# Zero rows of the decode tokens left out of DRAM and set on chip; z_b stored per block and channel in runs of 2 KB

## The chip, the cores and the metric

The kernel runs on one core of a Trainium2 chip. The metric is the device time of one execution in microseconds (us). Before the change it is 2897.08 us, the median of three runs (2893.88 to 2901.46).

## The reference, cut to what matters

One layer of a hybrid decoder, for 2048 prompt tokens and 8 decode tokens of one new position each, all in fp32. The layer projects the normalised input, mixes it in two branches, and projects back:

```
h    = rmsnorm(x, g_pre) * (1 + scale) + shift
u_a, v_a, z_a, x_b, z_b = split(h @ w_in)          # 5 x 1024 columns
y_a  = u_a * (tril(w_s) @ layernorm(v_a) + b_s) * silu(z_a)      # 8 heads, chunks of 128
h_t  = abar * h_(t-1) + bbar @ x_b[t]              # S5: 64 groups of 16 channels, 64 complex states each
g    = (Re(C h_t) + d * x_b[t]) @ w_glu + b_glu
y_b  = g[:16] * sigmoid(g[16:]) * silu(z_b)
out  = x + gate * rmsnorm(concat(y_a, y_b) @ w_out, g_post)
```

The prompt starts from a zero state. Each decode token starts from a given state and takes one step.

## The kernel before

**Blocks and column tiles.** The 2056 tokens stand on the free axis in four blocks (`blk`, `ranges`): 512 tokens in blocks 0 to 2, and 512 + 8 decode tokens in block 3, which is worked as 256 and 264 columns. TensorE multiplies in fp32r with both factors split in a high and a low part, so each product is three matmuls (`mm3`, L97 to L99). A column tile is 128 output channels of `h @ w_in`: 16 k-steps of three matmuls per range.

**Weights.** A half column tile of `w_in` (8 k-steps) comes in one 512 KB load into a raw tile `wraw` (L108; 3 buffers). ScalarE rounds it to `whi` (L90) and VectorE or GpSimd makes `wlo` (L85); there are 5 buffers (`NW`) of 4 k-steps each. A load waits for a free raw tile.

**Stages.** After the startup, the first stage makes x_b and z_b (8 column tiles of each, one per `e`), block by block from 0 to 3, up to about 870 us. `ev_xb` splits x_b in high and low parts and stores them to DRAM (`XB[e]`), ordered as channel, t, part, k, where a prompt token is 8k + t. `ev_zb` stores silu(z_b) (`ZB[e]`). Beside this stage `s5_mats` prepares the S5's matrices on GpSimd, ScalarE and VectorE in 16 rounds and stores them (PS, MQ, MT). The second stage makes v, z_a and u_a, block 3 first, then 0 to 2, up to about 2150 us, and the S5 runs inside it. The third stage is `@ w_out`.

**The S5.** Eight tokens (t) of 16 channels (c) are the 128 partitions of a tile, and k = 0 to 255 the columns; 8 further columns carry the decode tokens. `s5_u_mm` makes the state's inputs of a group from `xr` (128 x 2 x 272) and `pr`; `s5_scan` runs the recurrence over k on VectorE; `s5_y_load` loads, per group, `hr` (2 loads), `xr` again, `wr` (3 loads) and `zbl`; `s5_y_mm` does 12 matmuls, ScalarE, VectorE and GpSimd finish the tile `sg`, and it is stored to YB. In the S5's tiles a decode token is one column in which only one t is set: t = 7 where its inputs are made (columns 0 to 7 of the 272), t = 0 where its output is made (columns 264 to 271), and in `zbl` t = 0; the other seven rows are zero. The stores of block 3 (`dz`) write these columns to DRAM with their zeros, in runs of 8 numbers.

**What sets the order.** The code is emitted in program order by slots (`s5_steps`: 22 slots per `e`; in one half column tile of `phase1_rest` one slot is worked), and the tile framework then orders each engine's instructions by its own timeline model. Each engine runs its list in order; all DMAs are issued by SyncE (SP), in one list. There are eight DMA semaphores, used in turn, and a DMA waits until the one eight places before it has landed.

Of the kernel before, what the change touches and what calls it, by code (L numbers as in the profile page):

```python
# [28 lines left out]
GC = 16  # L29
P = 64  # L30
KT = D // 128
TC = 8
NK = L // TC
XW = NK + 2 * ND
HW = NK + ND
EPS = 1e-6
NE = 8
LEV = 5
MAGIC = 12582912.0
S5X, S5N = 4, 2  # L40
# [17 lines left out]
def ranges(b):  # L58

    return [(0, TB)] if b < NB - 1 else [(0, 256), (256, 264)]  # L60


class Builder:
# [330 lines left out]
    def ev_xb(self, b, e, acc):  # L394

        hi, lo = self.tile_(), self.tile_()
        hv, lv = (o[:, 0:TB].rearrange("p (t k) -> p t k", t=TC) for o in (hi, lo))
        for a, (r0, rn) in zip(acc, ranges(b)):
            m = min(rn, TB - r0)
            av = a[:, 0:m].rearrange("p (k t) -> p t k", t=TC)  # L400
            ks = slice(r0 // TC, (r0 + m) // TC)
            self.S.copy(hv[:, :, ks].bitcast(F32R), av)
            self.sub(self.V, lv[:, :, ks].bitcast(F32R), av, hv[:, :, ks])
        cols = slice(ND + b * 64, ND + b * 64 + 64)
        self.SP.dma_start(self.XB[e][:, :, 0, cols], hv)
        self.SP.dma_start(self.XB[e][:, :, 1, cols], lv)
        if b == NB - 1:
            dz = self.sp_.tile([128, 2, TC, 2, ND], F32, tag="dz", bufs=2, name=self.nm("dz"))
            self.G.memset(dz, 0.0)
            d = acc[1][:, 256:264]  # L410
            for i, t in ((0, TC - 1), (1, 0)):
                self.V.tensor_copy(dz[:, i, t, 0, :].bitcast(F32R), d)
                self.sub(self.V, dz[:, i, t, 1, :].bitcast(F32R), d, dz[:, i, t, 0, :])
            self.SP.dma_start(self.XB[e][:, :, :, 0:ND], dz[:, 0])
            self.SP.dma_start(self.XB[e][:, :, :, ND + NK : XW], dz[:, 1])

    def ev_zb(self, b, e, acc):
        o = self.tile_()
        ov = o[:, 0:TB].rearrange("p (t k) -> p t k", t=TC)
        for a, (r0, rn) in zip(acc, ranges(b)):  # L420
            m = min(rn, TB - r0)
            av = a[:, 0:m].rearrange("p (k t) -> p t k", t=TC)
            os_ = ov[:, :, r0 // TC : (r0 + m) // TC]
            self.S.activation(os_, av, AF.Sigmoid)
            self.V.tensor_mul(os_, os_, av)  # L425
        self.SP.dma_start(self.ZB[e].rearrange("t p k -> p t k")[:, :, b * 64 : b * 64 + 64], ov)
        if b == NB - 1:
            dz = self.sp_.tile([128, 2, TC, ND], F32, tag="dz", bufs=2, name=self.nm("dz"))
            self.G.memset(dz[:, 0], 0.0)
            self.S.activation(dz[:, 0, 0, :], acc[1][:, 256:264], AF.Sigmoid)  # L430
            self.V.tensor_mul(dz[:, 0, 0, :], dz[:, 0, 0, :], acc[1][:, 256:264])
            self.SP.dma_start(self.ZB[e].rearrange("t p k -> p t k")[:, :, NK:HW], dz[:, 0])

    def ev_v(self, b, j, acc):
        T, V, S = self.T, self.V, self.S
# [427 lines left out]
            SP.dma_start(mt[ti], kv[:, :, 32 * (TC - ti) : 32 * (TC - ti) + 256])  # L863


    def s5_x(self, e, gl):

        x = self.s5.tile([128, 2, XW], F32R, tag="s5x", bufs=S5X, name=self.nm("xr"))
        self.SP.dma_start(x.bitcast(F32), self.XB[e][gl * GC : gl * GC + GC].rearrange("c t h k -> (c t) h k"))
        return x  # L870

    def s5_u_load(self, e, gl):
        x = self.s5_x(e, gl)
        p = self.s5.tile([128, 2, 128], F32R, tag="s5p", bufs=S5N, name=self.nm("pr"))
# [75 lines left out]
    def s5_y_load(self, e, gl, r):  # L950
        SP, s5, nm = self.SP, self.s5, self.nm
        q, g2 = gl // 2, gl % 2
        h = s5.tile([128, 2, HW], F32R, tag="s5h", bufs=S5N, name=nm("hh"))
        self.split(r, h[:, 0], h[:, 1], self.V)
        x = self.s5_x(e, gl)
        w = s5.tile([128, 2, 2, 128, 2], F32R, tag="s5w", bufs=S5N, name=nm("wr"))
        mt = self.MT[e][gl // 4][q % 2].rearrange("t (h g c) n -> h g c t n", h=2, g=2)
        for hl in range(2):
            SP.dma_start(w[:, 0, hl].rearrange("p n e -> p (n e)").bitcast(F32), mt[hl, g2])
        SP.dma_start(w[:, 1].rearrange("p h n e -> p h (n e)").bitcast(F32), self.MQ[e][gl])  # L960
        zb = s5.tile([128, HW], F32, tag="s5z", bufs=S5N, name=nm("zbl"))
        SP.dma_start(zb, self.ZB[e][:, gl * GC : gl * GC + GC, :])
        return x, w, h, zb

    def s5_y_mm(self, e, gl, t):

        x, w, h, zb = t
        nm = self.nm
        g = e * 8 + gl
        mm = self.T.matmul  # L970
        xs = slice(ND, XW)
        po = []
        for hf in (1, 0):
            pg = self.ps.tile([128, 512], F32, tag="aux", bufs=4, name=nm("pg"))[:, 0:HW]
            po.append(pg)
            wm, wq = [w[:, 0, i, :, hf] for i in range(2)], [w[:, 1, i, :, hf] for i in range(2)]
            mm(pg, wm[0], x[:, 0, xs], start=True, stop=False)
            mm(pg, wm[0], x[:, 1, xs], start=False, stop=False)
            mm(pg, wm[1], x[:, 0, xs], start=False, stop=False)
            mm(pg, wq[0], h[:, 0, :], start=False, stop=False)  # L980
            mm(pg, wq[0], h[:, 1, :], start=False, stop=False)
            mm(pg, wq[1], h[:, 0, :], start=False, stop=True)
            if hf:
                yield
        sg = self.s5.tile([128, HW], F32, tag="sg", bufs=2, name=nm("sg"))
# [347 lines left out]
    def build(self):  # L1333
        nc, tc, I, V, G, SP = self.nc, self.tc, self.I, self.V, self.G, self.SP
# [29 lines left out]
        with tc.manual_schedule():  # L1364
            w, acc = self.startup(st, NG, nta)
# [186 lines left out]
```

## Time and profile before

| | |
|---|---|
| median of three runs | 2897.08 us |
| the profiled execution | 2893.71 us, span 2891.9 us, mean granted TensorE clock 0.995 |
| first stage (x_b, z_b) | to about 870 us |
| second stage (v, z_a, u_a and the S5) | about 870 to 2150 us |
| third stage (`@ w_out`) | about 2150 us to the end |
| DMA | 456704 packets, 581.22 MB |

The profile is of one execution. The engines are PE (TensorE's matmuls), PEld (its weight loads), DVE (VectorE), ACT (ScalarE), POOL (GpSimd) and SP (SyncE, which here only issues DMAs). The span runs from the first instruction to the last; some 2 us of the execution's time lie outside it. A busy PE is a PE with a matmul in flight; PEclk is the share of TensorE's full clock (2.4 GHz) that was granted.

### The profile page before, as it was taken

The numbers are of one execution on the slowest core, as the hardware profiler recorded it, in microseconds if no ns is written. First come the engines' busy times: TensorE is split into PE (matmuls) and PEld (weight loads), VectorE is DVE, ScalarE is ACT, GpSimd is POOL, SyncE is SP. The second block draws the span as 40 slices with busy tenths as digits, with TensorE's granted clock in tenths as the row PEclk, the third lists the DMA queues.
The fourth block names the chain that finished last, engine by engine and source line by source line (L and its number), as shares of the span: only waits on it lengthen the run. The fifth ranks groups of instructions, "written<-read, shape, count | busy, mean of one in ns | idle before, by whom it ended". The sixth has DMA issues, their size and how long they took to land.

```text
span 2891.9 us, 44349 instructions
## 1 busy us (share of the span) xinstructions
PE 2826.6 (98%) x15804; PEld 2375.1 (82%) x15804; DVE 1586.6 (55%) x2931; ACT 1065.5 (37%) x2008; POOL 1046.4 (36%) x973
## 2 busy tenths in 40 slices
PE   7999999999999999999999999999999999999998
PEld 4676777778899999988887888888888888888986
DVE  5467656465342837565546735482741174372866
ACT  3334444434233232433333332433243343434543
POOL 1128562662331232323232233223234345363443
PEclk9999999999999999999999999999999999999999
DMA  9898998987887373836476565637483365474676
GB/s 365 285 248 231 267 255 233 287 228 207 191 204 209 102 239 123 269 129 209 143 236 187 153 201 178 211 125 237 134 254 107 98 179 181 118 232 120 193 244 226
DMA packets 456704, 581.22 MB, mean 201 GB/s; under 512 B 216609, under 2 KB 303265, under 8 KB 456481
## 3 DMA queue, kind: packets, MB, share of 16 engines
q1 hardware_dynamic: 456482, 578.38, 66.9%
q8 instruction: 124, 2.03, 0.3%
q14 instruction: 98, 0.80, 0.1%
HBM read 466.94 MB, written 102.66 MB: 197 GB/s over the span
## 4 chain that ended last, share of the span: by engine, by line
PE 77%; DVE 10%; DMA 6%; issue 2%; SPq 2%; POOL 2%; ACT 1%; DVEq 0%; ACTq 0%; POOLq 0%
PE acc L97 23%; PE acc L99 23%; PE acc L98 22%; DVE Ub L899 2%; DVE wlo L85 2%; DMA wraw<-in_win 2%; PE ada L271 1%; DMA wraw<-in_woutr 1%; DVE sct L909 1%; DVE Ub L908 1%; DMA x<-in_xT 1%; DVE sct L907 1%; DVE Ub L910 1%; DMA wr<-MQ 1%; PE mix L531 1%
## 5 line engine op out<-in xcount | busy, mean ns | idle before, releaser
L97 PE MATMUL acc<-hi,whi 128*128 128x512 f32 (+2 forms) x3200 | 1132.6, 355 | 4.2 <-DVE t L425 2.6
L99 PE MATMUL acc<-hi,wlo 128*128 128x512 f32 (+2 forms) x3200 | 1121.2, 351 | 4.0 <-DVE wlo L85 3.7
L98 PE MATMUL acc<-lo,whi 128*128 128x512 f32 (+2 forms) x3200 | 1119.9, 350 | 3.8 <-DVE lo L375 3.5
L90 ACT CAST whi<-wraw 128x512 fp32r<-128x512 f32 x960 | 581.4, 620 | 1130.6 <-PE acc L98 796.4
L85 DVE TENSOR_TENSOR wlo<-wraw,whi 128x512 fp32r<-128x512 f32 x626 | 538.8, 867 | 826.0 <-ACT whi L90 794.8
L85 POOL TENSOR_TENSOR wlo<-wraw,whi 128x512 fp32r<-128x512 f32 x334 | 473.3, 1419 | 1054.7 <-ACT whi L90 960.6
L97 PEld LDWEIGHTS acc<-hi,whi 128*128 128x128 f32 x3200 | 604.1, 189 | 99.9 <-issue 19.4
L99 PEld LDWEIGHTS acc<-hi,wlo 128*128 128x128 f32 x3200 | 603.4, 189 | 91.2 <-DVE wlo L85 6.6
L98 PEld LDWEIGHTS acc<-lo,whi 128*128 128x128 f32 x3200 | 604.3, 189 | 80.2 <-DVE lo L375 6.7
L97 PE MATMUL acc<-yhi,whi 128*128 128x512 f32 (+1 forms) x1024 | 376.9, 369 | 2.8 <-DVE o L1074 2.8
L99 PE MATMUL acc<-yhi,wlo 128*128 128x512 f32 (+1 forms) x1024 | 375.0, 367 | 2.0 <-POOL wlo L85 2.0
L98 PE MATMUL acc<-ylo,whi 128*128 128x512 f32 (+1 forms) x1024 | 375.9, 367 | 0.0
L97 PEld LDWEIGHTS acc<-yhi,whi 128*128 128x128 f32 x1024 | 193.2, 189 | 38.4 <-DVE o L1074 3.6
L99 PEld LDWEIGHTS acc<-yhi,wlo 128*128 128x128 f32 x1024 | 192.8, 189 | 36.3 <-POOL wlo L85 2.4
L98 PEld LDWEIGHTS acc<-ylo,whi 128*128 128x128 f32 x1024 | 193.1, 189 | 34.5 <-issue 0.7
L899 DVE SCALAR_TENSOR_TENSOR Ub<-Ub,apow 128x128 f32<-128x128 f32 (+6 forms) x384 | 143.2, 438 | 2.5 <-ACT Ub L886 2.2
L988 POOL TENSOR_TENSOR sg<-sg,zbl 128x264 f32<-128x264 f32 x64 | 54.7, 854 | 192.3 <-DVE sg L987 124.6
L90 ACT CAST hh<-hr 128x264 fp32r<-128x264 f32 x64 | 26.3, 413 | 191.6 <-DMA hr<-Ub 97.5
L1077 POOL TENSOR_TENSOR ossq<-ossq,osq 128x512 f32<-128x512 f32 (+1 forms) x60 | 81.8, 1363 | 32.1 <-ACT osq L1070 31.9
L338 POOL TENSOR_TENSOR ssq<-ssq,t 128x512 f32<-128x512 f32 (+1 forms) x45 | 62.3, 1384 | 73.2 <-ACT t L337 72.5
L375 DVE SCALAR_TENSOR_TENSOR lo<-x,shiftT,hi 128x512 fp32r<-128x512 f32 x96 | 86.8, 921 | 0.7 <-ACT hi L374 0.5
L374 ACT ACTIVATE hi<-x,shiftT 128x512 fp32r<-128x512 f32 x96 | 67.3, 721 | 50.8 <-DVE x L373 42.9
(288 smaller groups left out, 2753.2 us busy)
## 6 DMA issues: line engine op xcount, KB each, us to landing
wraw<-in_win SPq DMA_DIRECT2D x320, 512.0 KB
wraw<-in_wout SPq DMA_DIRECT2D x128, 512.0 KB
xr<-XB SPq DMA_DIRECT2D x128, 272.0 KB
x<-in_xT SPq DMA_DIRECT2D x128, 256.0 KB
wraw<-in_wss SPq DMA_DIRECT2D x64, 512.0 KB
XB<-t SPq DMA_DIRECT2D x64, 256.0 KB
wraw<-in_wgt SPq DMA_DIRECT2D x32, 512.0 KB
MQ<-qh SPq DMA_DIRECT2D x128, 128.0 KB
```

Source lines behind the costliest of these rows:

```text
L85: eng.tensor_tensor(out, a, b, op=ALU.subtract)
L90: self.S.copy(hi, raw)
L97: mm(acc, whi, xhi, start=start, stop=False)
L98: mm(acc, whi, xlo, start=False, stop=False)
L99: mm(acc, wlo, xhi, start=False, stop=stop)
L271: self.T.matmul(ps[k * 32 : k * 32 + 32, 0:256], self.stat[:, q * 4 + k, :], raw[:, k * 256 : k * 256 + 256], start=q == 0, stop=q == 3)
L338: add_eng.tensor_tensor(ssq[:, 0:n], ssq[:, 0:n], sq[:, 0:n], op=ALU.add)
L374: S.activation(hi[:, 0:TB], xt, AF.Identity, bias=self.shiftT[:, k, 0:1])
L375: V.scalar_tensor_tensor(lo[:, 0:TB], xt, self.shiftT[:, k, 0:1], hi[:, 0:TB].bitcast(F32), op0=ALU.add, op1=ALU.subtract)
L899: V.scalar_tensor_tensor(o, i, f, o, op0=ALU.mult, op1=ALU.add)
L988: self.G.tensor_tensor(sg, sg, zb, op=ALU.mult)
L1077: eng.tensor_tensor(ssq[:, 0:nn], ssq[:, 0:nn], sq[:, 0:nn], op=ALU.add)
```

## The change

The decode columns of x_b and of silu(z_b) go to small DRAM tensors of their own, XD and ZD, without zeros. The S5's tiles have 264 columns where `xr` had 272: `s5_x` takes `tau` (7 for the input side, 0 for the output side), GpSimd sets the 8 decode columns of the tile to zero, one DMA loads the 256 prompt columns and another loads the 16 partitions of the decode columns that aren't zero. `ZB[e]` is now ordered as block, channel, t, k: a store writes 2 KB per channel, and a group's `zbl` is loaded in four DMAs of 32 KB, one per block, and one of ZD.

```diff
@@ ev_xb
-        cols = slice(ND + b * 64, ND + b * 64 + 64)
+        cols = slice(b * 64, b * 64 + 64)
...
-            dz = self.sp_.tile([128, 2, TC, 2, ND], F32, tag="dz", bufs=2, name=self.nm("dz"))
-            self.G.memset(dz, 0.0)
+            dz = self.sp_.tile([128, 2, ND], F32, tag="dz", bufs=2, name=self.nm("dz"))
             d = acc[1][:, 256:264]
-            for i, t in ((0, TC - 1), (1, 0)):
-                self.V.tensor_copy(dz[:, i, t, 0, :].bitcast(F32R), d)
-                self.sub(self.V, dz[:, i, t, 1, :].bitcast(F32R), d, dz[:, i, t, 0, :])
-            self.SP.dma_start(self.XB[e][:, :, :, 0:ND], dz[:, 0])
-            self.SP.dma_start(self.XB[e][:, :, :, ND + NK : XW], dz[:, 1])
+            self.V.tensor_copy(dz[:, 0, :].bitcast(F32R), d)
+            self.sub(self.V, dz[:, 1, :].bitcast(F32R), d, dz[:, 0, :])
+            self.SP.dma_start(self.XD[e], dz)
@@ ev_zb
-        self.SP.dma_start(self.ZB[e].rearrange("t p k -> p t k")[:, :, b * 64 : b * 64 + 64], ov)
+        self.SP.dma_start(self.ZB[e][b], ov)
...
-            dz = self.sp_.tile([128, 2, TC, ND], F32, tag="dz", bufs=2, name=self.nm("dz"))
-            self.G.memset(dz[:, 0], 0.0)
...
-            self.SP.dma_start(self.ZB[e].rearrange("t p k -> p t k")[:, :, NK:HW], dz[:, 0])
+            dz = self.sp_.tile([128, ND], F32, tag="dzz", bufs=2, name=self.nm("dz"))
...
+            self.SP.dma_start(self.ZD[e], dz)
@@ s5_x
-    def s5_x(self, e, gl):
-        x = self.s5.tile([128, 2, XW], F32R, tag="s5x", bufs=S5X, name=self.nm("xr"))
-        self.SP.dma_start(x.bitcast(F32), self.XB[e][gl * GC : gl * GC + GC].rearrange("c t h k -> (c t) h k"))
+    def s5_x(self, e, gl, tau):
+        x = self.s5.tile([128, 2, HW], F32R, tag="s5x", bufs=S5X, name=self.nm("xr"))
+        gs = slice(gl * GC, gl * GC + GC)
+        p0, d0 = (ND, 0) if tau else (0, NK)
+        xf = x.bitcast(F32)
+        self.G.memset(xf[:, :, d0 : d0 + ND], 0.0)
+        self.SP.dma_start(xf[:, :, p0 : p0 + NK], self.XB[e][gs].rearrange("c t h k -> (c t) h k"))
+        self.SP.dma_start(xf[tau::TC, :, d0 : d0 + ND], self.XD[e][gs])
@@ s5_y_load
-        SP.dma_start(zb, self.ZB[e][:, gl * GC : gl * GC + GC, :])
+        self.G.memset(zb[:, NK:HW], 0.0)
+        gs = slice(gl * GC, gl * GC + GC)
+        for b in range(NB):
+            SP.dma_start(zb[:, b * 64 : b * 64 + 64], self.ZB[e][b, gs].rearrange("c t k -> t c k"))
+        SP.dma_start(zb[0:GC, NK:HW], self.ZD[e][gs])
@@ build
+        self.XB = [dt_([128, TC, 2, NK], f"XB{e}") for e in range(NE)]
+        self.XD = [dt_([128, 2, ND], f"XD{e}") for e in range(NE)]
+        self.ZB = [dt_([NB, 128, TC, NK // NB], f"ZB{e}") for e in range(NE)]
+        self.ZD = [dt_([128, ND], f"ZD{e}") for e in range(NE)]
```

The order on GpSimd moves in block 3 of the first stage. Before, its list there holds the zeroing of `dz` (16 in all, L409 and L429) between the steps of `s5_mats` (F, mu, sc and ks are its tiles):

```order
L766 TENSOR_TENSOR dw_7216<-glw_7103,dd_7105 32x64
L409 MEMSET dz_7184 128x256
L766 TENSOR_TENSOR F_7375<-sc_7214,pw 128x576
L766 TENSOR_TENSOR mu_7195<-sc_7214,pw 128x576
L409 MEMSET dz_7354 128x256
L768 TENSOR_TENSOR F_7375<-F_7375,mu_7195 128x576
L824 TENSOR_SCALAR sc_7214<-sc_7214 128x128
L857 MEMSET ks_7556 64x2x256
```

After the change the same steps of the same round stand there alone:

```order
L761 TENSOR_TENSOR dw_7220<-glw_7111,dd_7113 32x64
L852 MEMSET ks_7552 64x2x256
L761 TENSOR_TENSOR F_7375<-sc_7218,pw 128x576
L761 TENSOR_TENSOR mu_7199<-sc_7218,pw 128x576
L763 TENSOR_TENSOR F_7375<-F_7375,mu_7199 128x576
L819 TENSOR_SCALAR sc_7218<-sc_7218 128x128
```

The 16 zeroings of `dz` are gone from GpSimd's list in the first stage; `ks` has moved ahead of the steps on F.

The order on SP moves where the S5's output groups are loaded. Before, between two loads of `wraw` in the S5 of `e` = 4, this is the beginning of the list (25 DMAs stand between the two loads):

```order
L108 DMA wraw_17613<-in_win 128x1024
L869 DMA xr_17602<-XB_61 128x544
L959 DMA wr_17467<-MT_0_137 128x1x256 x2
L960 DMA wr_17467<-MQ_125 128x512
L947 DMA hr_17543<-Ub 64x264
L989 DMA YB_77<-sg_17454 8x16x264
L962 DMA zbl_17471<-ZB_69 128x1x264
L959 DMA wr_17537<-MT_1_138 128x1x256 x2
L989 DMA YB_77<-sg_17521 8x16x264
```

After the change the same place reads as follows, and 49 DMAs stand between the two loads of `wraw`:

```order
L107 DMA wraw_17935<-in_win 128x1024
L869 DMA xr_17917<-XB_61 128x2x256
L960 DMA wr_17770<-MT_0_153 128x1x256 x2
L961 DMA wr_17770<-MQ_141 128x512
L948 DMA hr_17858<-Ub 64x264
L993 DMA YB_93<-sg_17755 8x16x264
L966 DMA zbl_17774<-ZB_77 128x1x64 x4
L967 DMA zbl_17774<-ZD_85 16x8
L993 DMA YB_93<-sg_17829 8x16x264
```

One load of `zbl` has become five, and each load of `xr` is followed, here or a few places on, by one of XD. SP's list has 2491 DMAs where it had 2115. In the S5 the longest stretch between two loads of `wraw` has 63 DMAs (it had 39; the first `e`), and in each of the seven other `e` there is one of 47 or 49 DMAs, where before three of them had one of 25 and none of the others had as many as 18.

On GpSimd's list in the second stage the zeroings of the decode columns (128 of `xr`, 64 of `zbl`) now stand between the products `sg` and the subtractions `wlo`:

```order
L992 TENSOR_TENSOR sg_11409<-sg_11409,zbl_11229 128x264
L963 MEMSET zbl_12562 128x8
L868 MEMSET xr_11532 128x2x8
L84 TENSOR_TENSOR wlo_11248<-wraw_11245,whi_11247 128x512
L868 MEMSET xr_11609 128x2x8
L992 TENSOR_TENSOR sg_11503<-sg_11503,zbl_11342 128x264
L84 TENSOR_TENSOR wlo_11358<-wraw_11355,whi_11357 128x512
```

Before, only the `sg`, the `wlo` and the products `t` of the gMLP stood there.

## Rows read from the trace of the kernel before

**Rows 1.** The page's first part: busy us, share of the span, instructions.
```profile
PE 2826.6 (98%) x15804; PEld 2375.1 (82%) x15804; DVE 1586.6 (55%) x2931; ACT 1065.5 (37%) x2008; POOL 1046.4 (36%) x973
```
**Rows 2.** Stretches of 50 us: busy us by engine, clock, DMA share, GB/s.
```profile
core 0: us, PE busy (x) PEld busy (x) DVE busy (x) ACT busy (x) POOL busy (x), PEclk, DMA share, GB/s
800.00:850.00 50.00, 46.21 (x368) 45.03 (x368) 22.94 (x37) 17.46 (x42) 26.53 (x34) 0.93 0.86 208
1000.00:1050.00 50.00, 49.71 (x413) 49.35 (x414) 25.71 (x63) 16.51 (x33) 16.72 (x15) 1.00 0.66 203
```
**Rows 3.** Stretches of 10 us within the first stage's end, same columns.
```profile
770.00:780.00 10.00, 5.67 (x47) 5.46 (x46) 4.77 (x6) 2.95 (x7) 7.32 (x7) 0.98 0.92 189
780.00:790.00 10.00, 8.72 (x70) 8.20 (x70) 3.70 (x12) 2.96 (x7) 5.23 (x11) 0.85 0.93 239
810.00:820.00 10.00, 6.21 (x42) 5.55 (x41) 6.13 (x7) 3.10 (x8) 9.45 (x12) 0.86 0.83 218
820.00:830.00 10.00, 10.00 (x80) 9.66 (x80) 6.82 (x13) 5.61 (x15) 4.79 (x7) 0.80 1.00 249
```
**Rows 4.** The chain of waits, 740 to 830 us: start us, us, what.
```profile
762.64 0.56 SPq L415
...
768.87 3.26 DMA MT<-ks
...
772.44 0.52 POOL ks L857
...
802.08 6.15 DMA XB<-dz
...
808.37 0.15 POOL dz L429
```
**Rows 5.** The tile `dz`: duration ns min/median/max, start us; then who waited.
```profile
L414 SPq DMA_DIRECT2D XB<-dz x8: 519/3314/4984, 708.0 to 798.4; - x8
L415 SPq DMA_DIRECT2D XB<-dz x8: 945/2339/3101, 711.9 to 802.1; - x8
L429 POOL MEMSET dz<- x8: 151/152/157, 796.9 to 876.9; 128x64 f32 x8
L432 SPq DMA_DIRECT2D ZB<-dz x8: 377/567/872, 818.7 to 899.5; - x8
...
  POOL dz L429: 54.0, 8
  POOL dz L409: 43.8, 6
```
**Rows 6.** Waits of TensorE, 870 to 2150 us: total us, times, longest.
```profile
PE acc L99 <- DVE wlo L85: 1.7, 2, 1.5
PE pg L980 <- DMA wr<-MQ: 1.3, 3, 0.8
PE vt L448 <- ACT t L439: 0.6, 2, 0.4
```
**Rows 7.** SP's queue in order of time, from 1000 us: start us, us, what.
```profile
1001.08 9.87 SPq L108 DMA_DIRECT2D wraw<-in_win  x4
...
1042.02 0.45 SPq L108 DMA_DIRECT2D wraw<-in_win  x1
```
**Rows 8.** SP's queue in order of time, from 1150 and 1329 us.
```profile
1160.03 0.33 SPq L108 DMA_DIRECT2D wraw<-in_win  x1
...
1167.33 0.33 SPq L108 DMA_DIRECT2D wraw<-in_win  x1
...
1329.22 0.34 SPq L108 DMA_DIRECT2D wraw<-in_win  x1
...
1348.77 1.55 SPq L108 DMA_DIRECT2D wraw<-in_win  x3
```
**Rows 9.** Issues on SP: duration ns min/median/max, first and last start us.
```profile
L962 SPq DMA_DIRECT2D zbl<-ZB x64: 587/609/679, 883.5 to 2120.8; - x64
L869 SPq DMA_DIRECT2D xr<-XB x128: 315/396/1588, 874.8 to 2103.8; - x128
```

More of the change, by code (lines that the diff above doesn't have):

```diff
@@ L33 @@
 NK = L // TC
-XW = NK + 2 * ND
 HW = NK + ND
@@ L425, in ev_zb @@
             self.V.tensor_mul(os_, os_, av)
-        self.SP.dma_start(self.ZB[e].rearrange("t p k -> p t k")[:, :, b * 64 : b * 64 + 64], ov)
+        self.SP.dma_start(self.ZB[e][b], ov)
         if b == NB - 1:
-            dz = self.sp_.tile([128, 2, TC, ND], F32, tag="dz", bufs=2, name=self.nm("dz"))
-            self.G.memset(dz[:, 0], 0.0)
-            self.S.activation(dz[:, 0, 0, :], acc[1][:, 256:264], AF.Sigmoid)
-            self.V.tensor_mul(dz[:, 0, 0, :], dz[:, 0, 0, :], acc[1][:, 256:264])
-            self.SP.dma_start(self.ZB[e].rearrange("t p k -> p t k")[:, :, NK:HW], dz[:, 0])
+            dz = self.sp_.tile([128, ND], F32, tag="dzz", bufs=2, name=self.nm("dz"))
+            self.S.activation(dz, acc[1][:, 256:264], AF.Sigmoid)
+            self.V.tensor_mul(dz, dz, acc[1][:, 256:264])
+            self.SP.dma_start(self.ZD[e], dz)
     def ev_v(self, b, j, acc):
@@ L863, in s5_mats @@
             SP.dma_start(mt[ti], kv[:, :, 32 * (TC - ti) : 32 * (TC - ti) + 256])
-    def s5_x(self, e, gl):
-        x = self.s5.tile([128, 2, XW], F32R, tag="s5x", bufs=S5X, name=self.nm("xr"))
-        self.SP.dma_start(x.bitcast(F32), self.XB[e][gl * GC : gl * GC + GC].rearrange("c t h k -> (c t) h k"))
+    def s5_x(self, e, gl, tau):
[6 more added lines that the diff above has]
+        self.SP.dma_start(xf[tau::TC, :, d0 : d0 + ND], self.XD[e][gs])
         return x
     def s5_u_load(self, e, gl):
-        x = self.s5_x(e, gl)
+        x = self.s5_x(e, gl, TC - 1)
         p = self.s5.tile([128, 2, 128], F32R, tag="s5p", bufs=S5N, name=self.nm("pr"))
@@ L882, in s5_u_mm @@
         ps = self.ps.tile([128, 512], F32, tag="aux", bufs=4, name=self.nm("pu"))
-        self.mm3(ps[:, 0:HW], p[:, 0], p[:, 1], x[:, 0, 0:HW], x[:, 1, 0:HW], True, True)
+        self.mm3(ps[:, 0:HW], p[:, 0], p[:, 1], x[:, 0], x[:, 1], True, True)
         q, g2 = gl // 2, gl % 2
@@ L954, in s5_y_load @@
         self.split(r, h[:, 0], h[:, 1], self.V)
-        x = self.s5_x(e, gl)
+        x = self.s5_x(e, gl, 0)
         w = s5.tile([128, 2, 2, 128, 2], F32R, tag="s5w", bufs=S5N, name=nm("wr"))
@@ L970, in s5_y_mm @@
         mm = self.T.matmul
-        xs = slice(ND, XW)
         po = []
@@ L976, in s5_y_mm @@
             wm, wq = [w[:, 0, i, :, hf] for i in range(2)], [w[:, 1, i, :, hf] for i in range(2)]
-            mm(pg, wm[0], x[:, 0, xs], start=True, stop=False)
-            mm(pg, wm[0], x[:, 1, xs], start=False, stop=False)
-            mm(pg, wm[1], x[:, 0, xs], start=False, stop=False)
+            mm(pg, wm[0], x[:, 0], start=True, stop=False)
+            mm(pg, wm[0], x[:, 1], start=False, stop=False)
+            mm(pg, wm[1], x[:, 0], start=False, stop=False)
             mm(pg, wq[0], h[:, 0, :], start=False, stop=False)
@@ L1340, in build @@
         dt_ = lambda s, n: dp.tile(s, F32, name=n, tag=n)
-        self.XB = [dt_([128, TC, 2, XW], f"XB{e}") for e in range(NE)]
-        self.ZB = [dt_([TC, 128, HW], f"ZB{e}") for e in range(NE)]
+        self.XB = [dt_([128, TC, 2, NK], f"XB{e}") for e in range(NE)]
+        self.XD = [dt_([128, 2, ND], f"XD{e}") for e in range(NE)]
+        self.ZB = [dt_([NB, 128, TC, NK // NB], f"ZB{e}") for e in range(NE)]
+        self.ZD = [dt_([128, ND], f"ZD{e}") for e in range(NE)]
         self.YB = [dt_([TC, 128, HW], f"YB{e}") for e in range(NE)]
@@ L1436, in build @@
         self.hpo = self.s5.tile([128, 2, 32], F32, name="hpo")
-        self.Ub = self.s5.tile([128, 2, 4, XW], F32, name="Ub")
+        self.Ub = self.s5.tile([128, 2, 4, NK + 2 * ND], F32, name="Ub")
         steps = self.s5_steps()
```

## The prediction

> **What bounds the kernel now.** I read the page's first part first, then the table of 50 us stretches, then in the two places that the change touches the 10 us stretches, the chain of waits and SP's queue. The first part shows TensorE busy for 2826.6 of 2891.9 us, and no other engine above 55% [rows 1]. So the end is set by how long TensorE stands still or runs at a lower clock, and an edit on another engine counts only where it makes or ends such a stretch. There is little to win: 65 us in all, most of it in the startup and at the end, where nothing of the change lies.
>
> Two stretches matter. At the end of the first stage TensorE stands still twice and its clock falls after each: busy 5.67 and 8.72 of 10 us from 770 us, 6.21 from 810 us, with a granted clock of 0.98, 0.85, 0.86 and 0.80 in the four rows [rows 3]. (The full clock is 2.4 GHz, and the lower level 1.2 GHz; these shares are a mixture of the two.) In the second stage, where the S5's tiles are loaded, it hardly waits: the three waits listed sum to 3.6 us in 1280 us [rows 6].
>
> **The first stage: what goes.** The stores of `dz` in block 3 go to DRAM in runs of 8 numbers. Their 16 issues hold SP for a median of 3.3 and 2.3 us each [rows 5], where another store or load holds it for 0.4 to 0.6 us [rows 9]. GpSimd zeroes the next `dz` only when such a store has landed, and it stood 43.8 and 54.0 us at these zeroings [rows 5]. Both stalls have a piece of it in their chain. Before the first one SP issues a store of `dz` (L415) and behind it the stores of `ks`; the landing of one of these (3.26 us) lets GpSimd's zeroing of `ks` and with it the round of `s5_mats` begin, and VectorE, which waits for that round, is late with the copies TensorE wants. Before the second one the landing of a `dz` store (6.15 us) holds GpSimd's zeroing at 808.37 us, and the same follows [rows 4].
>
> After the change this zeroing isn't there, a column tile has one small store to XD in place of two long ones, and VectorE makes 16 fewer small pieces. What it can give back is at most the two stalls: idle time of 4.33 + 1.28 + 3.79 = 9.4 us, and of the clock 0.02 x 5.67 + 0.15 x 8.72 + 0.14 x 6.21 + 0.20 x 10 = 4.3 us [rows 3], so 13.7 us. The second stall should go whole (3.79 + 0.87 + 2.0 = 6.7 us). The first has the landing of a `ks` store in it, which remains, only earlier by the time that SP is not held; I take half of its 4.33 + 1.28 + 0.11 + 1.31 = 7.0 us. That makes **-10 us**, between -14 and 0. What is late next in that stretch is the `ks` store itself, or the weights: SP's and GpSimd's lists lose work there and gain none, so I see no loss.
>
> The store of `ov` keeps its count and its issuing instruction; only its runs grow from 256 bytes to 2 KB. TensorE waits for no such store. I put it at 0.
>
> **The second stage: what comes.** Per group of the S5 there are six more DMAs: one of XD at the input side, one at the output side, and five for `zbl` where one stood. All go through SP's one list, and the loads of `wraw` stand in that list too. So the question is how long SP takes from one load of `wraw` to the next, and how long TensorE can go on meanwhile.
>
> The trace has one long stretch to measure this by. The last of four loads ends its issue at 1001.08 + 9.87 = 1010.95 us, and the next begins at 1042.02 us [rows 7]: 31.1 us for 39 DMAs (0.80 us each, waits included). In the 50 us around it TensorE was busy for 49.71 [rows 2], and the 0.3 us that is missing is at most what this cost. So TensorE can go on for at least 31.1 us without a new load. At most it can go on for what the buffers hold: three raw tiles and five pieces of half a raw tile are 5.5 half column tiles, at 7.3 us each (1160.03 to 1167.33 us, two loads in step with TensorE [rows 8]) 40 us, from which landing and splitting are still to be taken. Between the ends, 31.1 and 40, I take the middle, 36 us.
>
> In the changed list the same stretch has 63 DMAs, 24 more: 15 for `zbl`, 5 of ZD, 4 of XD. I price the 15 as the whole `zbl` was priced, since they have its number of partitions and so its pattern (0.609 us), and the small ones as a load of `xr` (0.396 us, the nearest row of a short issue) [rows 9]: 9.1 + 3.6 = 12.7 us. The bounds are 24 x 0.396 = 9.5 and, at the stretch's own 0.80 us, 19.1 us. The stretch then takes 43.8 us (40.6 to 50.2), which is 8 us more than TensorE can go on: **+8 us** (0.6 to 19). In each of the seven other `e` there is now a stretch of 47 or 49 DMAs. Before, 25 of them took 1348.77 - 1329.56 = 19.2 us [rows 8]; with 24 more at the same mean price (12.7 / 24) it is 31.9 us (28.7 to 38). Against 36 us this costs nothing, against 31.1 us up to 7 us each. I take 0.6 us each, **+4 us** (0 to 48).
>
> How long the DMAs take is a second limit, since eight can be on their way: for each DMA in the list the one eight places before must have landed. The row that bears on it is again the 31.1 us for 39 DMAs, in which 0.80 us each is more than SP's issues alone. The Trainium skill, "DMA: Bandwidth & Descriptors", section "Anatomy of one DMA", gives each DMA some 2.0 us that do not depend on its size (on GpSimd's path; no run here shows it for SP's). By it, as an estimate, 24 DMAs over eight places would add 24 x 2.0 / 8 = 6 us, less than the issues do, and the stall in the first `e` would be 1 us in place of 8. I go by the rows.
>
> GpSimd gets 192 short zeroings. At 152 ns, as the like one before [rows 5], they are 29 us of an engine that is busy for 36% [rows 1]; that cover is there everywhere in the stage. The danger is their wait: a zeroing of `xr` waits until TensorE has done with the tile that had this buffer, and behind it in GpSimd's list stand `wlo` pieces, for which TensorE waits. As `xr` has four buffers, the tile in question is long used; I put it at 0. The nearest row to its upper end is the wait at `dz`, which cost at most the 13.7 us above.
>
> The scheduler has also moved instructions in places that the change doesn't touch; I give that 0, and 3.6 us to either side, which is what TensorE waited in the whole second stage.
>
> **Sum.** -10 + 8 + 4 = +2 us. The profiled execution took 2893.71 us, so 2896; the median of the three runs lies 3.4 us higher, so **2899 us**.
>
> **Rivals.** A measurement of this kernel can tell a change of about 0.3% (8.7 us) from none.
>
> *SP's list becomes the bound in every burst of output loads.* If TensorE's reach is near 31 us, the first `e` costs 12.7 us and the others, between 0.8 and 7, some 3 us each: 34 - 10 = +24 us, 2921 us. It decides from a reach below some 34 us. For it: after landing and splitting, 40 us of buffers may well be no more than that, and SP's order keeps a store or load that waits for TensorE ahead of the next `wraw`. Against it: the 31.1 us went by at no cost, and SP's list lets several loads of `wraw` follow each other right after each burst.
>
> *The relief wins.* Both stalls go whole (-13.7 us) and the second stage loses nothing, its reach being near 40 us and the small DMAs cheap: 2883 us. For it: the `dz` rows are in both chains. Against it: the first `e` would have to stay within its reach with 24 DMAs more.
>
> *The relief doesn't come.* The landing of `ks` holds the same chain, which gives -2 us in place of -10, and the loads cost their 12: +10, 2907 us. For it: `ks` stands in the chain of the first stall, and GpSimd's list puts it ahead of F now. Against it: the second stall begins at a landing of `dz`.
>
> **How the numbers follow.** My forecast, the two terms nearly cancelling, gets 0.42; SP's list 0.22; the relief 0.25; no relief 0.11. So faster by over 0.3% 0.25, within 0.3% 0.42, slower 0.33. The forecast's own range is 2890 to 2908 us. The range reaches to both outer rivals, 2882 to 2924 us; outside are the upper ends of the unknown prices together.
>
> **What would show it.** Right: in the stretch from 750 to 830 us TensorE's busy time is nearly full and the clock 1.00, and `dz` is gone from GpSimd's waits; the longest pause between two loads of `wraw` is near 44 us, at about 1010 us, with some 8 us of idle TensorE behind it whose releaser is a `whi` or `wlo` piece; the seven other pauses are near 32 us with next to nothing behind them. Wrong: idle time of TensorE behind each of the eight bursts (the first rival), or the stalls near 775 and 815 us still there (the third), or a pause of 44 us that costs nothing (the second). If the issue of a piece of `zbl` takes well under 0.6 us, the prices of the second stage were too high.

## The result, and the profile after

The changed kernel took **2947.77 us** (median of 4 runs, 2945.88 to 2954.7), against 2899.14 us for the kernel before on the same chip: a ratio of **1.0179** (95% interval [1.0166, 1.0193], as in all ratios below), 49 us slower. The forecast was 2899 us, in a range of 2882 to 2924.

The page's first part of the changed kernel answers to [rows 1]: TensorE is busy for longer (the same matmuls at a lower clock) in a longer span (2952.6 us), and no other engine has come near it.

```profile
PE 2858.5 (97%) x15804; PEld 2392.6 (81%) x15804; DVE 1620.5 (55%) x2915; ACT 1064.1 (36%) x2008; POOL 1066.0 (36%) x1149
```

The stretches of the changed kernel (columns as in [rows 2]), with the S5 stage in one row at the end:

```profile
750.00:800.00 50.00, 50.00 (x430) 48.16 (x429) 24.98 (x40) 16.45 (x37) 24.48 (x32) 1.00 0.81 216
800.00:850.00 50.00, 50.00 (x429) 49.48 (x428) 21.17 (x40) 18.27 (x43) 19.28 (x27) 1.00 0.66 196
1000.00:1050.00 50.00, 42.71 (x345) 41.47 (x344) 15.40 (x34) 12.88 (x26) 13.74 (x28) 0.95 0.53 150
1050.00:1100.00 50.00, 49.23 (x390) 48.77 (x391) 16.46 (x29) 17.18 (x37) 14.20 (x20) 0.95 0.79 242
1350.00:1400.00 50.00, 44.75 (x217) 36.96 (x215) 11.34 (x17) 12.40 (x27) 12.41 (x24) 0.93 0.62 183
2000.00:2050.00 50.00, 44.94 (x211) 37.36 (x210) 12.19 (x17) 12.66 (x27) 12.95 (x25) 0.90 0.64 187
900.00:2250.00 1350.00, 1307.37 (x7204) 1128.61 (x7203) 752.58 (x1580) 434.95 (x812) 396.48 (x484) 0.98 0.57 172
```

The same stage of the kernel before:

```profile
900.00:2250.00 1350.00, 1346.07 (x7542) 1169.61 (x7541) 733.81 (x1594) 459.44 (x852) 401.93 (x318) 1.00 0.58 179
```

Two things are to be seen. The end of the first stage is full at full clock, so its relief came whole. And the S5 stage, which was idle for 3.9 us, is now idle for 42.6 us, with the clock down in eight places, some 160 us apart, one for each `e` (two of the eight are shown, and the first `e` in the two rows from 1000 us). Added up over 10 us stretches (busy time by what the granted clock lacks to 1.00) the clock takes another 20.2 us of this stage.

TensorE's waits, 870 to 2150 us, which answer to [rows 6]: more than half of the new ones are for `whi`, ScalarE's copy of a loaded weight; most of the others are for the S5's own tiles (`xr`, `wr`) and for GpSimd.

```profile
PE acc L96 <- ACT whi L89: 21.4, 12, 3.2
PE pu L96 <- DMA xr<-XD: 5.0, 4, 4.3
PE acc L98 <- POOL xr L868: 4.0, 4, 1.6
PE pg L981 <- DMA wr<-MT: 2.5, 5, 0.9
```

One burst shows why. SP's queue in order of time from 1338 us, which answers to the last group of [rows 8]:

```profile
1339.55 0.34 SPq L107 DMA_DIRECT2D wraw<-in_win  x1
1341.97 0.57 SPq L869 DMA_DIRECT2D xr<-XB  x1
...
1373.52 0.58 SPq L107 DMA_DIRECT2D wraw<-in_win  x1
...
1382.65 0.57 SPq L107 DMA_DIRECT2D wraw<-in_win  x1
...
1386.55 0.42 SPq L107 DMA_DIRECT2D wraw<-in_win  x1
```

What ScalarE and TensorE do with the load of 1373.52 us (all engines in order of time; in brackets the idle time before, and what ended it):

```profile
1378.71 1.14 ACT L89 CAST whi<-wraw 128x512 fp32r<-128x512 f32 x2 [1.71 <-DMA wraw<-in_win]
...
1379.38 0.80 PE L96 MATMUL acc<-hi,whi 128*128 128x512 f32 x1 [3.17 <-ACT whi L89]
```

And the clock around it, in stretches of 10 us:

```profile
1370.00:1380.00 10.00, 6.76 (x35) 5.39 (x33) 1.69 (x4) 2.68 (x6) 1.60 (x5) 0.97 0.64 171
1380.00:1390.00 10.00, 9.70 (x37) 7.66 (x36) 1.23 (x1) 0.36 (x1) 0.80 (x2) 0.69 0.77 228
```

From the end of one issue (1339.89) to the next load (1373.52) SP works off 49 DMAs in 33.6 us. Its own waits from 1340 to 1374 us sum to 4.6 us, and none of them is for the landing of a DMA; this is the longest:

```profile
SPq L869 <- PE pg L986: 2.4, 1, 2.4
```

So most of the pause is issues, one behind the other.

TensorE runs dry at 1379.38 - 3.17 = 1376.2 us, 36.3 us after the last load. But a load helps only when it has landed and is copied, which here takes from 1373.52 to 1379.38, 5.9 us. So the load had to be issued within 36.3 - 5.9 = 30.4 us, and it came 3.2 us late, which is the stall. The next 10 us run at a granted clock of 0.69, a mixture of 2.4 and 1.2 GHz, worth another 3.0 us.

And the next load comes only 13 DMAs later, where before three loads followed the burst together ([rows 8], x3). In four of the eight `e` TensorE's wait for `whi` falls at this second load and not at the first. One of them, after a pause of 31.3 us with 47 DMAs that caused no wait for `whi`; 16 DMAs stand between the two loads (SP and TensorE, in order of time):

```profile
1514.62 0.57 SPq L107 DMA_DIRECT2D wraw<-in_win  x1
...
1525.73 0.58 SPq L107 DMA_DIRECT2D wraw<-in_win  x1
...
1531.20 0.50 PE L96 MATMUL acc<-hi,whi 128*128 128x512 f32 x1 [2.83 <-ACT whi L89]
```

In the first `e` the larger wait is not for a weight at all. It is for the decode columns of `xr`, an S5 tile whose load stands in the same list:

```profile
1046.64 0.56 PE L96 MATMUL pu<-xr,pr 128*128 128x264 f32 x1 [4.32 <-DMA xr<-XD]
...
1049.78 0.58 PE L96 MATMUL acc<-hi,whi 128*128 128x256 f32 x1 [2.14 <-ACT whi L89]
```

### The profile page after: what moved, and what is told of

It reads as the page before. It is cut to its first block, busy times and chain, and to the rows that moved or that the text cites. A ratio compares the mean times of both kernels' runs of the same rounds, so it can differ in the third digit from the quotient of the medians.

```text
span 2952.6 us, 45042 instructions
## 1 busy us (share of the span) xinstructions
PE 2858.5 (97%) x15804; PEld 2392.6 (81%) x15804; DVE 1620.5 (55%) x2915; ACT 1064.1 (36%) x2008; POOL 1066.0 (36%) x1149
## 4 chain that ended last, share of the span: by engine, by line
PE 75%; DVE 11%; DMA 6%; issue 3%; SPq 3%; ACT 1%; POOL 1%; DVEq 0%; ACTq 0%; POOLq 0%
PE acc L96 22%; PE acc L98 22%; PE acc L97 22%; DVE Ub L900 2%; DVE wlo L84 2%; DMA wraw<-in_win 2%; PE ada L270 1%; DVE sct L910 1%; PE mix L526 1%; DVE Ub L909 1%; DVE sct L908 1%; DVE Ub L911 1%; PE acc L1232 1%; DMA wraw<-in_woutr 1%; PE acc L1231 1%
## 5 line engine op out<-in xcount | busy, mean ns | idle before, releaser
L84 DVE TENSOR_TENSOR wlo<-wraw,whi 128x512 fp32r<-128x512 f32 x626 | 567.9, 914 | 780.0 <-ACT whi L89 740.5
L868 POOL MEMSET xr<- 128x16 f32 x128 | 14.1, 111 | 249.1 <-PE pg L983 116.5
L372 DVE SCALAR_TENSOR_TENSOR x<-x,GT,R 128x512 f32<-128x512 f32 x96 | 80.3, 870 | 30.2 <-DMA x<-in_xT 30.0
L991 DVE SCALAR_TENSOR_TENSOR sg<-pg,c_bglu,sg 128x264 f32<-128x264 f32 x64 | 31.4, 491 | 108.3 <-PE pg L986 57.0
```

The source lines that it names most:

```text
L84: eng.tensor_tensor(out, a, b, op=ALU.subtract)
L372: V.scalar_tensor_tensor(xt, xt, self.GT[:, k, 0:1], R[:, 0:TB], op0=ALU.mult, op1=ALU.mult)
```

## The experiments

The theory after the result was the **list theory**: the number of DMAs between two loads of `wraw` in SP's one list makes the weights late. Its first rival was the **zeroing theory**: GpSimd's 192 zeroings wait for TensorE and hold the `wlo` pieces behind them (the 4.0 us at `xr L868` above). "Pause" is the time between two loads of `wraw` on SP; "idle" is TensorE's idle time from 900 to 2250 us. Ratios are to the kernel before, on the same chip.

| kernel | more DMAs on SP in the S5 | longest pauses, us | idle, us | time, us | ratio |
|---|---|---|---|---|---|
| before | 0 | 31.1; 3 near 18 | 3.9 | 2895 to 2899 | 1 |
| zeroings alone | 0 | 27.1; 3 near 18 | 4.7 | 2898.26 | 1.0007 [0.9998, 1.0017] |
| x part alone | 128 | 33.9; 3 of 23.5 | 6.8 | 2888.63 | 0.9971 [0.9961, 0.9981] |
| before, `zbl` in four | 192 | 40.4; 3 of 29, 4 of 22 | 8.4 | 2904.88 | 1.0027 [1.0017, 1.0037] |
| change, `zbl` in one | 192 | 37.2; 3 of 26.4 | 15.9 | 2900.19 | 1.0009 [0.9999, 1.0019] |
| z part alone | 256 | 43.4; 7 of 29 to 33 | 17.0 | 2916.88 | 1.0063 [1.0048, 1.0078] |
| change | 384 | 45.3; 7 of 30 to 34 | 42.6 | 2947.77 | 1.0179 [1.0166, 1.0193] |
| before, 384 more DMAs | 384 | 45.5; 7 of 30 to 34 | 48.7 | 2968.55 | 1.0243 [1.0218, 1.0268] |

### The two parts, each alone

```
x part alone:  XB without zero rows, XD, xr zeroed and set on chip; ZB as before
z part alone:  ZB per block and channel, ZD, five loads per zbl;    XB as before
```

> The x part of the change alone: decode rows in XD, zeroed and set into xr on chip; ZB and zbl as before. List theory (the number of DMAs between two loads of wraw on SP decides): at most 43 DMAs between two such loads in the first e and 33 in three others, where the changed kernel has 63 and 47 to 49 in all eight. At the changed kernel's 0.70 us per DMA these are pauses of 30 and 23 us, near those of before, so the S5 stage loses next to nothing, and with most of the first stage's relief the time is 2890 us (2884 to 2899). Zeroing theory (GpSimd's zeroing of xr waits for TensorE and holds the wlo pieces behind it): all 128 of the xr zeroings are here, so at least two thirds of the changed kernel's loss stay: 2925 us or more, with idle TensorE of some 25 us in the S5 stage.

> The z part alone: ZB per block and channel, five loads for a zbl, decode rows in ZD; XB and xr as before. List theory: 59 DMAs between two loads of wraw in the first e and 45 or 46 in the seven others, nearly those of the changed kernel, so pauses of 41 and 32 us and most of the loss: 2935 us (2920 to 2948). Zeroing theory: only the 64 zeroings of zbl are here, a third: 2910 us. In both the two stalls at the end of the first stage are shorter, not gone, since dz of x is still stored as before.

The stretch from 900 to 2250 us with the x part alone:

```profile
900.00:2250.00 1350.00, 1343.24 (x7454) 1163.20 (x7453) 732.49 (x1587) 457.13 (x847) 417.33 (x440) 1.00 0.57 176
```

The x part alone is **faster** than the kernel before, by 8 us, as the list theory had it: it has the whole relief of the first stage (TensorE busy for 200.00 us from 700 to 900 us) and two thirds of the zeroings, at hardly any idle time. The z part alone is slower by 18 us, half of what was expected and below the range given. Its pauses are as long as expected; but at 29 to 33 us most of them lie about the 30.4 us worked out above, and of these seven only the longest, 32.6 us, has a wait for `whi` at the first load behind it (1.3 us). Its largest waits from 870 to 2150 us are for an S5 tile and for `whi`:

```profile
PE pg L980 <- DMA wr<-MT: 6.1, 7, 1.8
PE acc L97 <- ACT whi L90: 5.5, 4, 2.5
```

The parts sum to 10 us and the change costs 49: they add to one list, and its cost begins only beyond a limit.

### The zeroings alone, and zbl in four pieces

```
+        self.G.memset(x.bitcast(F32)[:, :, d0 : d0 + ND], 0.0)
...
+        self.G.memset(zb[:, NK:HW], 0.0)
```
The zeroings alone stand ahead of the loads of before. And `zbl` in four:
```
-        SP.dma_start(zb, self.ZB[e][:, gl * GC : gl * GC + GC, :])
+        for b in range(NB):
+            n = 64 if b < NB - 1 else 64 + ND
+            SP.dma_start(zb[:, b * 64 : b * 64 + n], self.ZB[e][:, gl * GC : gl * GC + GC, b * 64 : b * 64 + n])
```

> The kernel before, with the 192 zeroings of the change set ahead of its loads of xr and zbl, which then overwrite the zeros; no DMA more, layouts and stores as before. List theory: 40 DMAs between loads of wraw in the first e, 25 in three others, as before, so no loss: 2898 us (2893 to 2904). Zeroing theory: GpSimd's list with the zeroings in it, and each load now waits for its zeroing: the loss of the changed kernel, or two thirds of it, 2930 us or more.

> The kernel before, with each zbl loaded by four DMAs in place of one, from the old layout, zero rows included: nothing is zeroed on chip and nothing of the first stage changes. List theory: 54 DMAs between two loads of wraw in the first e, 42 in three and 33 in four others; at 0.70 us pauses of 38, 29 and 23 us: slower than before, by less than the change, about 2918 us (2908 to 2930), with idle TensorE behind the long pauses alone. Zeroing theory: no zeroing, so no loss: 2899 us.

With the zeroings alone:

```profile
900.00:2250.00 1350.00, 1345.29 (x7523) 1168.43 (x7522) 727.86 (x1589) 460.33 (x853) 419.27 (x504) 1.00 0.58 179
```

The zeroing theory falls: 192 zeroings, each ahead of a load that waits for it, cost nothing that can be measured. So the waits at `xr L868` in the changed kernel need its fuller list as well. Four pieces of `zbl` cost 7 us with nothing zeroed, where 19 was expected (it lies below the range given): its seven shorter pauses, 22 to 30 us, lie below the 30.4 us, and no wait for `whi` follows any of them; the 40.4 us of the first `e` has one of 2.7 us.

### One thing taken back: zbl by one load

```
-        self.SP.dma_start(self.ZB[e][b], ov)
+        self.SP.dma_start(self.ZB[e].rearrange("t p k -> p t k")[:, :, b * 64 : b * 64 + 64], ov)
...
-        for b in range(NB):
-            SP.dma_start(zb[:, b * 64 : b * 64 + 64], self.ZB[e][b, gs].rearrange("c t k -> t c k"))
+        SP.dma_start(zb[:, 0:NK], self.ZB[e][:, gs, :])
...
```

> The changed kernel with one thing taken back: ZB is kept in the old order of channels (without its zero rows), so that a zbl comes by one load and one of ZD in place of four and one. Every zeroing on chip and the whole relief of the first stage stay. List theory: 48 DMAs between two loads of wraw in the first e and 37 in three others, where the changed kernel has 63 and 47 to 49 in eight; at 0.70 us that is 34 and 26 us, as in the kernel with the x part alone, which was idle for 6.8 us in the S5 stage: 2890 us (2885 to 2896). Zeroing theory: all 192 zeroings are there, so the time stays near the changed kernel's: above 2930 us. Also told apart: in the sum of the two parts run alone the change would cost 18.0 - 8.4 = 10 us, but it costs 49; if both parts only add DMAs to one list, taking 12 of the 24 away must give back most of the 49.

Taking 12 of the 24 DMAs of four groups away gives back nearly all: 2900 us. It misses the 2890 by 10 and lies above the range given, because the stage stays idle for 15.9 us; there TensorE waits 6.3 us for `wlo` pieces of VectorE and 2.7 us for `wr`. Why this is twice what `zbl` in four pieces costs, with as many DMAs, stays open.

### The count alone

```
-        self.SP.dma_start(x.bitcast(F32), self.XB[e][gl * GC : gl * GC + GC].rearrange("c t h k -> (c t) h k"))
+        xb = self.XB[e][gl * GC : gl * GC + GC].rearrange("c t h k -> (c t) h k")
+        for p in (0, P):
+            self.SP.dma_start(x.bitcast(F32)[p : p + P], xb[p : p + P])
...
-        SP.dma_start(zb, self.ZB[e][:, gl * GC : gl * GC + GC, :])
+        for t0, t1 in ((0, 2), (2, 4), (4, 6), (6, 7), (7, 8)):
+            SP.dma_start(zb[t0 * GC : t1 * GC], self.ZB[e][t0:t1, gl * GC : gl * GC + GC, :])
```

> The kernel before with nothing but 384 more DMAs: each xr comes in two halves (by partitions) and each zbl in five pieces (by rows), from the layouts of before, with the same bytes in the same runs, nothing zeroed on chip, the first stage as before. SP's list then has the changed kernel's counts between loads of wraw, 63, 13, 47, 16, 13, 13, 49 and so on. List theory (the count on SP alone, by the weights behind it): the S5 stage loses as in the changed kernel, some 59 us, and there is no relief in the first stage: 2955 us (2935 to 2965). Rival (the changed kernel's short runs, its 8-number rows and the zeroings in a fuller list are what is slow): most of it is gone, below 2925 us.

The stage, and the first row of TensorE's waits from 870 to 2150 us, of the kernel before with 384 more DMAs:

```profile
900.00:2250.00 1350.00, 1301.32 (x7215) 1123.50 (x7215) 746.61 (x1581) 432.48 (x807) 377.56 (x296) 0.98 0.61 174
```
```profile
PE acc L97 <- ACT whi L90: 21.4, 13, 3.5
```

This is nearly the changed kernel's loss, with the same bytes and runs as before and nothing zeroed: 21.4 us for `whi` in both, 48.7 us idle in place of 42.6, and 15.9 us of clock in place of 20.2. TensorE even waits 3.8 us for `wlo` of GpSimd here, about what it waits at `xr L868` in the changed kernel. By the medians it takes 21 us more than the changed kernel and lies 4 us above the range given; 9 of these 21 are the first stage's stalls, which it still has (6.1 us idle and 2.8 us of clock from 700 to 900 us), and the rest has no row that shows it. So the number of DMAs is enough by itself.

### The weights on another list, and the zbl loads on another list

```
-        self.SP.dma_start(raw if len(src.shape) == 2 else raw.rearrange("p (a b) -> p a b", a=2), src)
+        q = self.S if tag == "wraw" and getattr(self, "part", 0) == 1 else self.SP
+        q.dma_start(raw if len(src.shape) == 2 else raw.rearrange("p (a b) -> p a b", a=2), src)
```

In one kernel `self.G` stands for `self.S`; in the last one the weights are left on SP, and it is `self.S.dma_start` that issues the five loads of `zbl` and ZD.

> The changed kernel with the loads of wraw in the second stage issued by ScalarE in place of SP; all else, the 24 more DMAs of each burst too, as changed. List theory (the weights are late because they stand behind the S5's DMAs in SP's one list): no load of wraw stands behind a burst any more, the eight waits of 2 to 3 us for whi go and with them the falls of the clock; what stays are the S5's own tiles, late on SP (xr and wr, 9 us of the 42.6 us of idle TensorE). About 2900 us (2888 to 2912). Rival, the transfers are what is slow: a wraw on another list lands as late: 2935 us or more. Third possibility: a load that waits for its raw buffer holds ScalarE, whose splits come late: also above 2920 us, but with idle TensorE spread over the stage, not behind the bursts.

> The control: the kernel before with the loads of wraw in the second stage issued by ScalarE. There the S5 stage is idle for 3.9 us only, so a free list has nothing to give: 2897 us (2893 to 2903) by the list theory. If ScalarE is held by these loads it is slower by as much as the changed kernel with the same move suffers, which then must be taken off.

> The same with GpSimd issuing the loads of wraw in the second stage. List theory: as with ScalarE, about 2900 us (2888 to 2912); GpSimd's issues are longer (1.1 us in the kernel with its stores of zeros) and stand beside its wlo pieces. Transfers: 2935 us or more.

> The x part alone, with the loads of wraw in the second stage issued by ScalarE. The x part alone took 2888.6 us and was idle for 6.8 us in the S5 stage, with 2.9 us lost to the clock. List theory: up to these 9 us less those of the kernel before, so 2884 us (2880 to 2890).

> The changed kernel with the five loads per group of zbl and ZD issued by ScalarE in place of SP: the same DMAs, bytes, runs and zeroings, another list. List theory: SP has 37 or 38 DMAs between loads of wraw, pauses of about 26 us, and the S5 stage is idle for less than 12 us: 2890 to 2900 us, if ScalarE, busy for 37%, carries 320 issues of 0.4 to 0.6 us without being late with its splits (whi). Rival, the transfers themselves (short runs, their number on the way, the DMA engines' share) make the weights late, whoever issues them: no change, 2940 to 2950 us. Zeroing theory: no change either.

The moved loads are those of the third stage too, which the expectations did not say. The changed kernel with the weights on ScalarE's list took 2915.94 us, 1.0071 [1.0055, 1.0087], 4 us above the range that the list theory gave. Its S5 stage, and TensorE's first waits from 870 to 2150 us:

```profile
900.00:2250.00 1350.00, 1325.20 (x7345) 1143.68 (x7345) 727.15 (x1582) 442.16 (x834) 400.94 (x495) 1.00 0.58 174
```
```profile
PE pg L982 <- DMA wr<-MT: 10.4, 5, 4.4
PE pg L985 <- DMA wr<-MQ: 3.6, 6, 1.9
PE pg L982 <- DMA zbl<-ZB: 3.4, 1, 3.4
```

The waits for `whi` are gone, all 21.4 us of them, and the clock stays up; what TensorE waits for now are the S5's own tiles, still on SP. The control was not free, against what was expected: the kernel before with the same move took 2908.44 us, 1.0049 [1.0034, 1.0064], and its S5 stage was idle for 16.5 us:

```profile
900.00:2250.00 1350.00, 1333.51 (x7451) 1157.48 (x7450) 729.37 (x1587) 450.28 (x845) 392.49 (x314) 1.00 0.57 177
```

So 7 of the 49 us between the kernels are left when both have their weights on another list; the other 40 or so are, by this difference, weights behind DMAs in one list. That figure is rough: the difference supposes that the move costs the same in every kernel, but it cost 13 us in the kernel before and 18 in the x part (below). On GpSimd's list the changed kernel took 2936.29 us, 1.0139 [1.0120, 1.0158]. By its time alone this would speak for the rival, slow transfers (2935 us or more), and the list theory's range is missed. But there is no wait for `whi` among the waits of the stage here either (idle 27.5 us), and it loses the rest mostly in the third stage (TensorE busy for 42.84 and 40.42 us in the two stretches from 2700 to 2800 us, before 44.88 and 49.17). The x part with the weights on ScalarE took 2906.93 us, 1.0045 [1.0029, 1.0062], where 2884 was expected: the move is no gain.

With the `zbl` and ZD loads on ScalarE's list the changed kernel took 2915.05 us, 1.0064 [1.0047, 1.0081]. That gives back two thirds, not all:

```profile
PE acc L96 <- ACT whi L89: 8.4, 6, 3.2
PE acc L98 <- POOL wlo L84: 4.9, 8, 0.9
```

The expected 2890 to 2900 us is missed. In the first `e` and three others SP's longest pauses are 33 to 38 us there, with 37 or 38 DMAs and not 49, some 0.9 us for each. SP now waits between its issues: from 1331 to 1364 us, which holds one of these pauses, its waits sum to some 10 us (4.6 in the changed kernel's burst above). The largest of them are for stores of `sg` that come behind zeroings of `zbl` on GpSimd:

```profile
SPq L993 <- POOL zbl L963: 3.0, 3, 1.6
```

The transfers are the same, so about two thirds of the changed kernel's loss do not come from the transfers alone.

### The relief without the loads

```
+        if b == 1:
+            self.SP.dma_start(self.XB[e][:, :, :, 0:ND], self.zz)
+            self.SP.dma_start(self.XB[e][:, :, :, ND + NK : XW], self.zz)
         if b == NB - 1:
...
+            self.SP.dma_start(self.XB[e][:, TC - 1, :, 0:ND], dz)
+            self.SP.dma_start(self.XB[e][:, 0, :, ND + NK : XW], dz)
```

`zz` is a tile of zeros that is set once; ZB's rows likewise. In the second kernel it is `b == 2` and `self.G`.

> The kernel before with its DRAM layouts and its loads in the S5 untouched; only the stores of the decode rows differ: the zero rows are written at block 1 from a tile of zeros that is set once, and block 3 stores the non-zero decode rows alone. If the first stage's relief is worth what the trace of the changed kernel shows there (9.4 us less idle and a full clock from 700 to 900 us), and the S5's loss comes from its loads alone, the time is 2887 us (2882 to 2892), better than both. Rival: the long stores of zeros hold SP for 2 to 3 us each at block 1 as they did at block 3, and the stall only moves there: 2899 us.

> As the kernel that writes its zeros at block 1, but the 24 stores of zeros are issued by GpSimd at block 2. Layouts and loads of the S5 as before. If what the long stores cost is SP's list being held, as the 24 stores within 36 us at block 1 held it (22.9 us of idle TensorE), the relief is now free and the time is 2886 us (2881 to 2893). If the DMA engines are what they block, the stall moves to block 2: 2905 us or more.

Both were wrong: 2922.38 us, 1.0086 [1.0069, 1.0103], and 2918.13 us, 1.0078 [1.0063, 1.0093]. Two stretches of 25 us of the first:

```profile
200.00:225.00 25.00, 9.52 (x37) 7.70 (x38) 10.89 (x35) 5.60 (x12) 16.11 (x24) 0.66 0.94 234
300.00:325.00 25.00, 14.78 (x61) 9.51 (x62) 24.90 (x28) 8.81 (x16) 19.75 (x21) 0.73 0.85 249
```

The stalls at 750 to 850 us are gone and the S5 is as before (idle 3.1 us), but stalls at 200 to 325 us cost more than that. The stores from GpSimd began at 141 us, since nothing holds them back to block 2, and TensorE lost as much (idle 31.5 us from 120 to 700 us, before 8.4). So taking these stores off SP's list gave nothing back; whether the DMA engines, the list that issues them or the work's new order decides wasn't settled.

## Why the prediction was wrong

**First stage, -10 us: right, at the upper end.** Both stalls are gone, 9.4 us of idle time and 4.3 us of clock, the whole 13.7 us. It came from the x part (the z part alone kept 7.7 us of idle time there); XD's stores still hold SP (below, L411), but TensorE loses no time by it.

**The prices of the new DMAs: right.** The changed kernel's issues (ns, minimum, median, maximum; first and last start us):

```profile
L966 SPq DMA_DIRECT2D zbl<-ZB x256: 567/580/1265, 877.8 to 2180.4; - x128
L967 SPq DMA_DIRECT2D zbl<-ZD x64: 323/399/481, 881.5 to 2181.1; - x64
```
```profile
L870 SPq DMA_DIRECT2D xr<-XD x128: 523/594/1829, 864.7 to 2176.0; - x128
```
```profile
L411 SPq DMA_DIRECT2D XD<-dz x8: 425/2223/3793, 711.7 to 786.6; - x8
```

15 x 0.580 + 5 x 0.399 + 4 x 0.594 = 13.1 us for the 24, against 12.7. The pauses were forecast at 43.8 us and 31.9 us and came at 45.3 and 30 to 34 us.

**The first burst, +8 us: right in idle time, in part by luck.** The two rows from 1000 us have 7.29 + 0.77 = 8.1 us, and the clock, added up over stretches of 10 us as above, takes another 3.3. But the prediction put all of it on weights (`whi` or `wlo`), and 4.3 us of it are the wait for the decode columns of `xr`, which the prediction did not have. The reach of 36 us was about right in this burst: pauses of 33.9, 37.2, 40.4, 43.4 and 45.3 us in five of the kernels were followed there by waits for `xr` and `whi` of 0, 1.0, 3.3, 5.6 and 6.5 us, so the limit was 36 to 39 us.

**The seven other bursts, +4 us: here the prediction failed.** "Against 36 us this costs nothing" set a pause of SP's issues against the time until TensorE runs dry. TensorE did run dry after 36 us (36.3 in the burst above), but landing and copying, 5.9 us of it, had been named and not taken off; the limit for an issue was 30.4 us there. The three pauses with 49 DMAs (33.3 to 34.0 us) lay beyond it, and in them TensorE waits 2.5 to 3.2 us for `whi` at the first load behind. The stage's other stretches were idle for 42.6 - 8.1 = 34.5 us, up to 3.9 of which were there before: over 30 us, not 4. That 31.1 us had cost nothing was true of the first `e` alone, where four loads stand together ahead of the pause [rows 7]; ahead of the others stands one [rows 8]. The pause was also looked at alone: the next load follows 13 or 16 DMAs later. The four pauses with 47 DMAs (29.6 to 31.9 us) passed without a wait for `whi`, and in just these four `e` TensorE waits 2.3 to 2.8 us for it at the second load.

**The clock was left out of this term.** Each of these stalls is followed by stretches at a lower granted clock, 20.2 us in the stage, 3.3 of them in the first burst. The first stage's term had counted it, the second's had not. The Trainium skill, "TensorE: Matmul & The Clock Gate", section "HAM oscillation — how this bites in real kernels", describes a kernel that waits for a transfer in every step and pays for the clock again each time. The eight bursts agree, with 0.69 over 10 us behind the stall shown.

**The rival with SP's list** had the mechanism and the place. It was priced at 3 us a burst, 2921 us, again without the clock.

**The sum.** -13.7 + 38.7 (idle in the S5) + 20.2 (clock) = +45 us; the medians differ by 49. The profiled execution was the longest of its four and differs by 61, and 11 us of its longer busy time have no row that I could find.

**At nothing, and rightly:** the zeroings, by their own run. The rule weighed in the prediction, the Trainium skill's "DMA: Bandwidth & Descriptors", section "Anatomy of one DMA", would have given a stall of 1 us in the first burst, by the estimate worked out there; the idle time was 8.1 us, near the 8 that the issue times gave, and SP waited for no landing in the burst shown above.

## What to carry to other kernels

When one list issues both bulk loads and loads with a due time, compare the time between two of the latter with what the buffers cover **less** landing and conversion, and do it for several loads in a row, not for the one long pause that the trace happens to show. Such a cost begins at a limit, so parts that are harmless alone can be dear together; and where the trace shows the clock falling behind TensorE's stalls, as here, a new stall is to be priced with it. Here the part that took long stores away without many new loads, the x part, was the version to keep: 0.9971 of the time before [0.9961, 0.9981], ahead of both.

## What the runs showed of the hardware

The issue of an `xr` took 0.550 us in the changed kernel (median), where it had taken 0.396 [rows 9]: the same count of bytes but for the zero columns, now set into a part of a wider tile. The shortest one rose from 0.315 to 0.521 us. How long an issue takes does not depend on its own pattern alone: the load of `wr` from MQ, which the change leaves as it was, took 0.439 us before and 0.580 after (medians). After a wait of TensorE of 3.2 us the granted clock was 0.69 over the next 10 us. But idle time does not always cost clock. In the kernel with the weights on GpSimd's list TensorE was idle for 27.5 us in the S5 stage, with waits of up to 3.1 us, at a granted clock of 1.00:

```profile
900.00:2250.00 1350.00, 1322.46 (x7356) 1141.14 (x7356) 743.64 (x1584) 445.06 (x834) 519.87 (x706) 1.00 0.58 175
```

And a load moved from SP's list to ScalarE's is not free for the others: in the kernel before, TensorE then waited 12.7 us for `wr`, which stayed on SP.
